# Two matmuls with a GELU between: b's first load cut in two, a first cast on two engines, and warm-up zeros from a constant

## The chip, the cores and the metric

The kernel runs on one NeuronCore of a Trainium2 chip. A core has a matrix engine (TensorE, PE in the profile; its weight loads are listed apart as PEld), a vector engine (VectorE, DVE), a scalar engine for activation functions (ScalarE, ACT), a general engine (GpSimd, POOL), a queue engine that here only issues transfers (SyncE, SP), and 16 DMA engines. The engines run their own instruction streams and wait for each other through semaphores. The metric is device time in microseconds (us), the median of several executions; less is better. A profiled execution has a span, from its first to its last instruction, and its own time, which is a little longer.

## The reference

```
h   = a @ b                      # a: 1024 x 1024, b: 1024 x 2048, float32
h   = 0.5*h*(1 + tanh(sqrt(2/pi)*(h + 0.044715*h**3)))
out = h @ c                      # c: 2048 x 1024, float32
```

## The kernel before

The order of all work is written out by hand: each engine does its instructions in the order in which the program lists them.

**Storage.** a comes to the core as float32 into `sta`, b's first 512 columns as float32 into `stb`; the rest of b and all of c come through POOL's queue, which converts them to bfloat16 on the way. The k axis (1024) is cut into eight slices of 128; `stb[:, k]` is slice k of b's first 512 columns, 256 KB.

**Loads.** All SP loads are issued at the start, in the order a piece, b pair, a piece, and again (lines 69 to 82). `load_a(h, q)` brings rows 512h to 512h + 511 of a and its columns 256q to 256q + 255; `load_b(q)` brings the two slices 2q and 2q + 1 of b. Each is 512 KB. `load_a(0, 0)`, `load_b(0)`, `load_a(1, 0)` are the first three. POOL's loads wait for a later piece of a through the one-element copy `gate` (line 84).

**Warm-up.** `stir` (lines 113 to 117) multiplies a tile of zeros, `warm`, with itself on PE, in passes of the given widths, into a PSUM bank that the first true product overwrites. It keeps PE at work while nothing has landed. `warm` is written by a DVE memset on line 50. A single-element Gelu on line 85 makes ACT load its table early.

**First stage.** For each piece of a, `cast_a` (119 to 125) converts float32 to bfloat16 (`ab`), on one or two engines, each taking a share of the 256 columns; `turn` (127 to 134) transposes it on PE in two groups of four and copies each group to `aT` with DVE. The second group goes to the same PSUM bank as the first. `cast_b` (136 to 139) converts a slice of b on ACT into `b1`, slice 0 in two halves. `block` then issues products of 128x512 on PE (line 105) for a row half, a set of column tiles and a set of slices. For the first pieces the order on PE is (lines 214 to 226):

```
stir(256, 256, 256, 256)
tn = turn(0, 0, 4, cast_a(0, 0, nc.vector))
next(tn)
stir(256)
next(tn)
stir(128)
cast_b(0, 2)
cast_b(1)
ab = cast_a(1, 0, nc.vector, nc.scalar)
block(0, range(4), (0,))
block(0, range(2), (1,))
tn = turn(1, 0, 7, ab)
next(tn)
```

So the six first products come before the transposes of a's second piece, and those before everything that follows.

**Later stages.** The other columns of the first matmul and the whole second one are done by a scheme with seven block products in place of eight (`Seven`, `seven`, lines 147 to 383): DVE forms sums and differences of blocks, PE multiplies them (line 197), DVE and ACT bring the results out of PSUM. `done2` stores the tiles of the output; the four tiles of the first quadrant go out in two halves each (line 443).

Of the kernel before, what the change touches and what calls it, by code (L numbers as in the profile page):

```python
# [9 lines left out]
F32 = mybir.dt.float32  # L10
F32R = mybir.dt.float32r
BF16 = mybir.dt.bfloat16
AF = mybir.ActivationFunctionType
# [6 lines left out]
def kernel(ctx, tc, a, b, c, out):  # L20
    nc = tc.nc
# [3 lines left out]
    H = 512  # L25
# [4 lines left out]
    bv = b.rearrange("(kt p) n -> p kt n", p=128)  # L30
# [3 lines left out]
    consts = ctx.enter_context(tc.tile_pool(name="consts", bufs=1))  # L34
# [5 lines left out]
    def slot(tag, shape, dt, name):  # L40
        return big.tile(shape, dt, name=name, tag=tag)

    def bank(i, shape=(128, H), dt=F32, name="ps"):
        return pp.tile(list(shape), dt, name=name, tag=f"bank{i}", padded_shape=None)

    def pieces(tag, bufs, shape, dt, name):
        return small.tile(shape, dt, name=name, tag=tag, bufs=bufs)

    warm = consts.tile([128, 256], F32, name="warm")
    nc.vector.memset(warm, 0.0)  # L50
    ident = consts.tile([128, 128], BF16, name="ident")
    make_identity(nc, ident)
    gate = consts.tile([128, 1], F32, name="gate")
    g = consts.tile([128, 1], F32, name="g")
# [11 lines left out]
    stb = slot("x0", [128, KT, H], F32, "stb")  # L66
    sta = [slot(f"x{i}", [128, 2, 2, 4, 256], F32, "sta") for i in (1, 3)]

    def load_a(h, q):
        nc.sync.dma_start(out=sta[q // 2][:, h, q % 2],  # L70
                          in_=av[:, 4 * h:4 * h + 4, ds(q * 256, 256)])

    def load_b(q):
        nc.sync.dma_start(out=stb[:, 2 * q:2 * q + 2], in_=bv[:, 2 * q:2 * q + 2, 0:H])

    load_a(0, 0)
    load_b(0)
    load_a(1, 0)
    for q in range(1, 4):
        load_a(0, q)  # L80
        load_b(q)
        load_a(1, q)

    nc.gpsimd.tensor_copy(gate, sta[1][:, 1, 0, 3, 0:1])
    nc.scalar.activation(g, warm[:, 0:1], AF.Gelu_apprx_tanh)


    for k in range(0, KT, 4):
# [1 line left out]
    for n in range(2):  # L90
        for k in range(0, KT, 4):
            nc.gpsimd.dma_start(out=b2[:, k:k + 4, ts(n, H)],
                                in_=bv[:, k:k + 4, ds(1024 + n * H, H)])
# [3 lines left out]
    def copy(eng, dst, src):  # L97
        if eng is nc.scalar:
            nc.scalar.activation(dst, src, AF.Copy)  # L99
        else:  # L100
            nc.vector.tensor_copy(dst, src)  # L101
# [11 lines left out]
    def stir(*widths):  # L113

        for w in widths:
            nc.tensor.matmul(ps[0, 3][:, 0:w], warm[:, 0:128], warm[:, 0:w],
                             start=True, stop=True, skip_group_check=True)

    def cast_a(h, q, *engs):

        ab = pieces("ab", 2, [128, 4, 256], BF16, "ab")
        for i, eng in enumerate(engs):
            w = 256 // len(engs)
            copy(eng, ab[:, :, ts(i, w)], sta[q // 2][:, h, q % 2][:, :, ts(i, w)])
        return ab

    def turn(h, q, i, ab):

        pt = bank(i, (128, 2, H), BF16, "pt")
        for n in range(2):  # L130
            for m in range(4):
                nc.tensor.transpose(pt[:, n, ts(m, 128)], ab[:, m, ts(n, 128)], ident)  # L132
            nc.vector.tensor_copy(aT[:, h, 2 * q + n], pt[:, n])  # L133
            yield

    def cast_b(k, n=1):
        for i in range(n):
            r = ds(i * (H // n), H // n)
            nc.scalar.activation(b1[:, k, r], stb[:, k, r], AF.Copy)  # L139
# [71 lines left out]
    zero = Seven(4, quarters(b1, H, 256), BB, [None] * 4, [None] * 4, 2)  # L211
    one = Seven(4, quarters(b2, 0, H), BB, [None] * 4, zero.t)

    stir(256, 256, 256, 256)
    tn = turn(0, 0, 4, cast_a(0, 0, nc.vector))
    next(tn)
    stir(256)
    next(tn)
    stir(128)
    cast_b(0, 2)  # L220
    cast_b(1)
    ab = cast_a(1, 0, nc.vector, nc.scalar)
# [2 lines left out]
    tn = turn(1, 0, 7, ab)  # L225
# [9 lines left out]
    tn = turn(0, 1, 7, ab)  # L235
# [8 lines left out]
    tn = turn(1, 1, 7, ab)  # L244
# [6 lines left out]
    tn = turn(0, 2, 7, ab)  # L251
# [8 lines left out]
    tn = turn(1, 2, 7, ab)  # L260
# [6 lines left out]
    tn = turn(0, 3, 7, ab)  # L267
# [13 lines left out]
    tn = turn(1, 3, 0, ab)  # L281
# [153 lines left out]
    def store(mt, q0, w, ot, eng=None):  # L435
        (eng or nc.sync).dma_start(out=out[ts(mt, 128), ds(q0, w)], in_=ot)

    def done2(i, l, j, p):
        if (i, l) == (1, 0):
            ot = pieces("o", 4, [128, H], F32, "ot")  # L440
            nc.vector.tensor_copy(ot, p)
            p = ot
        n = 2 if (i, l) == (0, 0) else 1
        for q in range(n):
            r = ds(q * (H // n), H // n)
            store(4 * i + j, l * H + q * (H // n), H // n, p[:, r])

    def between2(n):
# [12 lines left out]
        elif n == "P73":  # L461
            two.t4(two.t[1], 4)

    seven(two, done2, between2)


# [28 lines left out]
```

## Time and profile before

| | |
|---|---|
| Median of 13 runs | 118.22 us (117.94 to 119.35) |
| Profiled execution, its own time | 118.2 us |
| Its span | 116.4 us |
| PE busy | 111.1 us, 95% of the span |
| DVE busy | 90.5 us, 78% |
| ACT busy | 59.4 us, 51% |
| POOL busy | 11.0 us, 9% |
| SP's loads of a | 8 of 512 KB, 8.5 us from issue to landing |
| SP's loads of b | 4 of 512 KB, 8.1 us from issue to landing |
| First warm-up pass on PE | at 1.19 us |
| First product of the reference on PE | at 7.06 us |

A busy time is the sum over an engine's instructions; two engines are usually busy at once, so the rows don't add up to the span. The end of a PE instruction is modelled, and a busy PE isn't PE at its peak. A row of the trace gives start, length, engine, line, operation, operands, and in brackets the idle time of the engine before it with what ended that. The lines of the text are those of the kernel before.

### The profile page before, as it was taken

What the parts mean: (1) busy time and instruction counts of PE and PEld (TensorE: products, weight loads), DVE (VectorE), ACT (ScalarE), POOL (GpSimd) and SP (SyncE); (2) the same over time, 40 slices, a digit from 0 to 9 for tenths busy, and PEclk for the clock granted to TensorE, in tenths of its full rate; (3) what the DMA queues carried; (4) which work ended last, traced back from release to release, by engine and by line L of the source; (5) the groups of instructions that cost most, each with busy time, mean ns of one, the idle gap of its engine ahead of it and who ended that gap; (6) DMA issues with size and microseconds to landing.
All of it is one profiled execution on the core that took longest, in us unless ns stands there. A gap on an engine that the chain in (4) does not pass through costs nothing.

```text
span 116.4 us, 1478 instructions
## 1 busy us (share of the span) xinstructions
PE 111.1 (95%) x540; PEld 76.3 (66%) x540; DVE 90.5 (78%) x107; ACT 59.4 (51%) x99; POOL 11.0 (9%) x21
## 2 busy tenths in 40 slices
PE   5889999999999999999999999999999999999980
PEld 5544455545777447888886444588888888888860
DVE  0236666899998999844689999999999986954670
ACT  5066668989369898066699329600033982000000
POOL 2000049623322000000000000000000000000000
PEclk9999999999999999999999999999999999999999
DMA  3999999999999999997000000070000002014993
GB/s 87 292 376 391 395 395 312 204 207 207 204 210 213 211 212 210 212 210 150 3 0 0 0 6 0 2 268 0 0 0 0 0 0 96 0 63 174 368 361 115
DMA packets 13542, 17.91 MB, mean 154 GB/s; under 512 B 736, under 2 KB 8928, under 8 KB 13536
## 3 DMA queue, kind: packets, MB, share of 16 engines
q0 software_dynamic: 5344, 7.34, 35.5%
q1 hardware_dynamic: 8192, 10.49, 25.2%
q8 instruction: 4, 0.07, 0.2%
q14 instruction: 2, 0.02, 0.0%
HBM read 20.97 MB, written 4.19 MB: 216 GB/s over the span
## 4 chain that ended last, share of the span: by engine, by line
PE 91%; DMA 5%; DVE 1%; SPq 0%; ACT 0%; issue 0%
PE ps L197 76%; PE ps L105 12%; DMA stb<-in_b_dram 5%; PE pt L132 3%; DVE aT L133 0%; SPq L70 0%; ACT b L139 0%; DVE ot L382 0%
## 5 line engine op out<-in xcount | busy, mean ns | idle before, releaser
L197 PE MATMUL ps<-x,s 128*128 128x512 f32 x128 | 29.6, 391 | 0.0
L197 PEld LDWEIGHTS ps<-x,s 128*128 128x128 f32 x128 | 24.0, 188 | 5.1
L197 PE MATMUL ps<-x,x 128*128 128x512 f32 x96 | 22.9, 394 | 0.0
L197 PEld LDWEIGHTS ps<-x,x 128*128 128x128 f32 x96 | 18.0, 188 | 3.9
L105 PE MATMUL ps<-aT,b 128*128 128x512 bf16 x64 | 16.3, 379 | 0.3 <-ACT b L139 0.3
L305 ACT ACTIVATE v<-ps 128x512 f32<-128x512 f32 x10 | 6.0, 599 | 19.4 <-PE ps L197 19.4
L197 PE MATMUL ps<-c_sb,hT 128*128 128x512 bf16 (+1 forms) x72 | 14.2, 356 | 0.0
L197 PE MATMUL ps<-x 128*128 128x512 f32 x56 | 13.2, 392 | 0.0
L197 PEld LDWEIGHTS ps<-x 128*128 128x128 f32 x56 | 10.2, 188 | 2.6 <-ACT v L305 0.4
L197 PEld LDWEIGHTS <-hT 128*128 128x128 bf16 x72 | 6.9, 98 | 7.1 <-issue 0.5
L133 DVE COPY aT<-pt 128x512 bf16<-128x512 bf16 x16 | 6.8, 424 | 5.8 <-PE pt L132 5.8
L109 ACT ACTIVATE hT<-ot 128x512 bf16<-128x512 f32 x18 | 10.5, 625 | 1.5 <-DVE ot L310 1.1
L310 DVE TENSOR_TENSOR ot<-ps,v 128x512 f32<-128x512 f32 x10 | 6.7, 688 | 5.2 <-DMA out_dram<-ot 3.8
L310 DVE TENSOR_TENSOR ot<-ps,u 128x512 f32<-128x512 f32 x10 | 6.7, 691 | 5.1 <-ACT u L305 5.1
L197 PE MATMUL ps<-aT,b 128*128 128x512 bf16 x48 | 10.7, 379 | 0.0
L155 DVE TENSOR_TENSOR x<-c_sb 128x1024 fp32r<-128x1024 bf16 x8 | 9.3, 1225 | 0.0
L105 PEld LDWEIGHTS <-b 128*128 128x128 bf16 x64 | 5.5, 98 | 4.6 <-ACT b L139 0.9
L197 PEld LDWEIGHTS <-b 128*128 128x128 bf16 x48 | 4.6, 98 | 5.7 <-issue 0.3
L132 PEld LDWEIGHTS <-ab 128*128 128x128 bf16 x64 | 4.5, 97 | 5.9 <-DVE ab L101 2.1
L99 ACT ACTIVATE ab<-sta 128x512 bf16<-128x512 f32 x10 | 6.0, 625 | 3.5 <-DMA sta<-in_a_dram 3.4
L305 ACT ACTIVATE u<-ps 128x512 f32<-128x512 f32 x10 | 5.9, 598 | 3.3 <-PE ps L197 3.2
L109 ACT ACTIVATE hT<-ps 128x512 bf16<-128x512 f32 x14 | 7.3, 596 | 0.4 <-PE ps L105 0.3
(39 smaller groups left out, 114.3 us busy)
## 6 DMA issues: line engine op xcount, KB each, us to landing
sta<-in_a_dram SPq DMA_DIRECT2D x8, 512.0 KB, 8.5
c_sb<-in_c_dram POOLq DMA_DIRECT2D x8, 512.0 KB, 19.9
b<-in_b_dram POOLq DMA_DIRECT2D x6, 512.0 KB, 11.4
out_dram<-ot SPq DMA_DIRECT2D x12, 256.0 KB, 2.1
stb<-in_b_dram SPq DMA_DIRECT2D x4, 512.0 KB, 8.1
out_dram<-ot SPq DMA_DIRECT2D x8, 128.0 KB, 2.0
```

The costliest lines, as they stand in the source:

```text
L99: nc.scalar.activation(dst, src, AF.Copy)
L105: nc.tensor.matmul(p, b1[:, k, ts(t, 128)], aT[:, h, k], start=(k == 0), stop=(k == KT - 1))
L109: nc.scalar.activation(hT[h][:, t], p, AF.Gelu_apprx_tanh)
L132: nc.tensor.transpose(pt[:, n, ts(m, 128)], ab[:, m, ts(n, 128)], ident)
L133: nc.vector.tensor_copy(aT[:, h, 2 * q + n], pt[:, n])
L155: nc.vector.tensor_tensor(out=dst[:, r], in0=x[:, r], in1=y[:, r], op=op)
L197: nc.tensor.matmul(p[:, ds(c0, w)], l[:, k, ts(j, 128)], r[:, k, ds(c0, w)], start=(start and k == 0), stop=(k == self.kt - 1), skip_group ...
L305: nc.scalar.activation(st, p, AF.Copy)
L310: nc.vector.tensor_tensor(out=ot, in0=p, in1=st, op=ADD)
```

## The change

b's first load becomes two loads of one slice each, on the same queue; the warm-up reads its zeros from a constant that the program has anyway, so that tile and memset go; the table-loading Gelu stands ahead of the loads in the program; the first cast of a is shared by DVE and ACT; the warm-up passes have other widths; and the first output tile is stored whole.

```diff
-    warm = consts.tile([128, 256], F32, name="warm")
-    nc.vector.memset(warm, 0.0)
+    warm = nc.const_aps.tensor(0.0, [128, 256], F32)
...
+    def load_b0(k, eng):
+        eng.dma_start(out=stb[:, k], in_=bv[:, k, 0:H])
+
     def load_b(q):
         nc.sync.dma_start(out=stb[:, 2 * q:2 * q + 2], in_=bv[:, 2 * q:2 * q + 2, 0:H])
 
+    nc.scalar.activation(g, warm[:, 0:1], AF.Gelu_apprx_tanh)
     load_a(0, 0)
-    load_b(0)
+    load_b0(0, nc.sync)
+    load_b0(1, nc.sync)
     load_a(1, 0)
...
     nc.gpsimd.tensor_copy(gate, sta[1][:, 1, 0, 3, 0:1])
-    nc.scalar.activation(g, warm[:, 0:1], AF.Gelu_apprx_tanh)
...
-    stir(256, 256, 256, 256)
-    tn = turn(0, 0, 4, cast_a(0, 0, nc.vector))
-    next(tn)
-    stir(256)
+    stir(256, 256, 256, 256, 128)
+    tn = turn(0, 0, 4, cast_a(0, 0, nc.vector, nc.scalar))
     next(tn)
     stir(128)
+    next(tn)
+    stir(64)
     cast_b(0, 2)
...
-        n = 2 if (i, l) == (0, 0) else 1
+        n = 2 if (i, l) == (0, 0) and j else 1
```

## The prediction

> **What bounds the kernel now.** I read the busy row first, then the chain of waits in order of time, then the first 17 us engine by engine, because every edit but one lies there.
>
> The slices of the page say that TensorE (PE) is busy nearly all the time, while the DMA engines are full through about the first 23 us:
>
> ```profile
> PE   5889999999999999999999999999999999999980
> DMA  3999999999999999997000000070000002014993
> ```
>
> The chain that ended last gives the work on the path. Its pieces (start, length, what) include:
>
> ```profile
> 1.22 5.35 DMA stb<-in_b_dram
> ...
> 7.06 1.47 PE ps L105 x6
> ...
> 25.16 87.99 PE ps L197 x400
> ```
>
> Read naively this says: 5.35 us wait on b's first load, then nothing but PE to 113.2 us, so every tenth by which b comes sooner is a tenth off the end. The chain names only one releaser per step, however. I ask what the next wait would be if this one went, and read VectorE (DVE) and ScalarE (ACT) in the same stretch (start, length, line, operation, idle time before it and what ended it):
>
> ```profile
> 4.46 0.69 DVE L101 CAST ab<-sta 128x1024 bf16<-128x1024 f32 x1 [3.33 <-DMA sta<-in_a_dram]
> 5.64 0.42 DVE L133 COPY aT<-pt 128x512 bf16<-128x512 bf16 x1 [0.49 <-PE pt L132]
> 6.54 0.42 DVE L133 COPY aT<-pt 128x512 bf16<-128x512 bf16 x1 [0.47 <-PE pt L132]
> 7.95 0.43 DVE L101 CAST ab<-sta 128x512 bf16<-128x512 f32 x1 [0.98 <-DMA sta<-in_a_dram]
> ```
>
> The last row decides this case. DVE has been idle 0.98 us when it casts the second piece of a (rows 512 to 1023, load_a(1, 0)): that piece has only just landed, near 7.93. Its first transpose follows at once:
>
> ```profile
> 8.43 0.23 PEld L132 LDWEIGHTS <-ab 128*128 128x128 bf16 x4 [0.39 <-DVE ab L101]
> ```
>
> 7.95 + 0.43 = 8.38, and PE takes the cast piece at 8.43. So two chains meet at 8.4: b's first load through six products, and a's second piece through its cast. They are a tie. Later pieces of a gate PE too, by little:
>
> ```profile
> 9.63 1.15 ACT L99 ACTIVATE ab<-sta 128x512 bf16<-128x512 f32 x2 [1.06 <-DMA sta<-in_a_dram]
> 12.23 0.63 ACT L99 ACTIVATE ab<-sta 128x512 bf16<-128x512 f32 x1 [0.25 <-DMA sta<-in_a_dram]
> 16.28 0.63 ACT L99 ACTIVATE ab<-sta 128x512 bf16<-128x512 f32 x1 [0.27 <-DMA sta<-in_a_dram]
> ```
>
> PE transposes from these casts at 10.32, 12.71 and 16.78. What runs ahead of each is three, five and five products of 0.216 us (1.08 us for five in the chain): 9.56 + 0.65 = 10.21, 11.51 + 1.08 = 12.59, 15.67 + 1.08 = 16.75. PE therefore stands still for 0.11, 0.12 and 0.03 us, and could not gain more by being early. Up to about 16.8 us the clock of this kernel is the stream of loads; from there on it is PE's own work.
>
> That stream, by stretches of 1.5 us (PE, PEld, DVE, ACT and POOL busy, granted clock, DMA share, GB/s), is not even:
>
> ```profile
> 2.75:4.25 1.50, 1.50 (x5) 1.22 (x4) 0.00 (x0) 0.00 (x0) 0.00 (x0) 1.00 1.08 363
> 4.25:5.75 1.50, 1.02 (x8) 0.52 (x7) 0.80 (x2) 0.00 (x0) 0.00 (x0) 1.00 0.89 224
> 5.75:7.25 1.50, 1.19 (x9) 0.64 (x8) 0.74 (x2) 0.66 (x3) 0.00 (x0) 1.00 1.05 360
> 7.25:8.75 1.50, 1.50 (x11) 0.67 (x10) 0.43 (x1) 1.22 (x3) 0.00 (x0) 1.00 1.08 391
> ```
>
> While b's first load moves, the rate drops to 224 GB/s although the engines stay 0.89 busy. Against 391 that is (391 - 224) x 1.5 us = 250 KB, or 0.64 us. I cannot say why; it matters below.
>
> **What the skill says.** "DMA: Bandwidth & Descriptors", section "Queues, rings and completion order": on each DMA engine the descriptors of one queue are consumed in ring order, and a load's semaphore step lands after all earlier writes of that engine. The trace agrees: a's first piece, b's first load and a's second piece are waited for until 4.44, 6.57 and 7.93, in the order of issue. "Perfetto Trace Analysis", section "DMA Optimizations": splitting helps some work start sooner if the engines are generally idle. Here they are full, so the split only decides which bytes of b come first. "TensorE: Matmul & The Clock Gate", Part 1: PE starts at half rate, comes to full rate after about 3.4 us of activity, and may fall back after an idle window of that length. The trace agrees on the first half: eight passes of the warm-up take 3.55 us, two later ones of the same size 0.65 us, and no fall back shows. "ScalarE: Activation LUTs", "What ACT_TABLE_LOAD costs": 186 ns plus 0.833 ns an element, 613 ns for 512; the casts here take 613 to 630.
>
> **The change part by part.**
>
> *b's first load in two.* 512 KB become two loads of 256 KB on SP, slice k = 0 ahead. At 4.25 us the stream has moved 129 x 1.55 + 363 x 1.5 = 745 KB; slice 0 ends at 786 KB, so at 224 GB/s its data are in by 4.45. b's whole load (1,048 KB) is in by the same sum at 5.6 and is waited for until 6.57, one microsecond for the landing. Slice 0 then lands near 5.45, slice 1 near 6.57 as before.
>
> *First cast on two engines.* DVE does 128x512 in 0.43 instead of 128x1024 in 0.69, ACT the other half in 0.63: 4.46 to 4.89 and to 5.09. ACT is free, as it was idle 4.36 us up to 6.59. First transposes 0.26 sooner, at 4.94; the first aT copy ends near 5.80 instead of 6.06. The second group of transposes waits for that copy (same bank, as before), near 5.85.
>
> *Warm-up.* DVE's memset (0.27) goes, and PE need not wait until 1.19; the other engines start at 0.73, so PE gains some 0.4. Four 256-wide passes cost 3.55, the added 128-wide one half of 0.89, together 4.0: from 0.8 to 4.8, inside the wait for the first cast. The two later ones shrink by half, which saves about 0.2 each, hidden. Reading zeros from a broadcast constant isn't shown in the trace; I take the same rate, with 1 us more as the bad end, which the slack below covers in part.
>
> *Sum for the first product.* PE is through its second transposes and the small warm-up near 6.3; b's slice 0 is cast 5.47 to 6.25. First product near 6.35, not 7.06: 0.7 sooner. Slice 1 is cast 6.59 to 7.22, its first two products end near 7.7. Then PE reaches the transposes of a's second piece, which lands at 7.93 as before: it waits to 8.43. Of 0.7 us nearly all is lost in that wait. What remains is the bit by which PE was itself late at 8.43, at most 0.05.
>
> *SP's queue.* One issue more, 0.43 to 0.49 each; everything behind it (a's second piece and the rest) is issued some 0.4 later. a's second piece would be issued by about 2.7, and its first bytes move only after 1,048 KB, at 5.6, so 2.9 us of queue hide it. For later loads 8 us lie between issue and landing. Cost taken as 0; bounds 0 to +0.4.
>
> *The rest.* The Gelu that loads the activation table moves ahead of nothing on ACT (next work at 4.46, table and Gelu done at 2.22): 0. The first output tile goes out as one 256 KB store, not two: one SP issue of 0.35 less at 75 us, under a single unbroken PE piece from 25.16 to 113.15: 0. The removed tile shifts later addresses by 1 KB; nothing in the trace prices that: 0, bounds -0.1 to +0.1.
>
> Sum: -0.05 on a profiled span of 116.4, whose execution took 118.2 (1.8 outside the span) and is the median of 118.22 to within 0.02. Forecast 118.15.
>
> **The rivals.**
>
> *Faster: the stream itself gains.* The drop at 4.25 to 5.75 belongs to b's first load. If two loads of consecutive rows don't suffer it, or less, a's second piece lands up to 0.64 sooner, and since every later gate is a landing, all of it arrives at the end: 117.5 to 117.85. For it: the drop lies exactly on the load that is cut, and b's later loads ran at 391. Against: the bytes, row sizes and row pitch are the same.
>
> *Faster: the naive chain.* The full 0.7 would count, 117.5. The cast at 7.95 speaks against it.
>
> *Slower: PE's clock falls back.* Between 4.8 and 8.43 PE now works less: transposes 0.46, warm-ups 0.35, six products 1.3, some 2.1 of 3.6 us, where before it was some 2.6 of 3.7. If that counts as idle, products run at half rate for a window of 3.4 us after 8.43: up to +1.7, 119.2 to 119.9. It decides from the point where that stretch is under the limit; the trace shows none. One of the thirteen times before is 119.35, which such a fall back could explain.
>
> *Slower: the extra load delays the stream* by one issue, 0.4, if the DMA engines run dry behind it: 118.6.
>
> *It doesn't do what it says*, slice 0 landing with slice 1: also 118.2.
>
> **How the numbers follow.** About 0.3% (0.35 us) is what a measurement of this kernel can tell from no change. No change 0.42 (118.0 to 118.4 for its own part). Faster 0.36: stream 0.30, naive chain 0.06. Slower 0.22: clock 0.10, stream 0.12. The range 117.5 to 118.9 holds the stream's gain and loss and leaves out mostly the clock.
>
> **What would show it.** First product near 6.35; DVE's cast of a's second piece again near 7.95 after more than a microsecond of idle, and the six products no longer touching the transposes at 8.43; the cast pieces at 9.6, 12.2 and 16.3 in place. I am wrong if that cast starts 0.3 or more away from 7.95, either way: the end will move with it. If it stays and the end moves, the tie was misread, or PE's rate changed after 8.4.

## The result and the profile after

The changed kernel is slower: a median of 119.5 us (118.84 to 120.42, 11 runs) against 118.22 us (48 runs). The ratio is 1.0106, with a 95% interval of 1.0089 to 1.0123. Its profiled execution took 118.84 us with a span of 117.0 us. That is its fastest run, so the profile shows 0.64 us of a loss that is 1.28 us in the median. What it shows of the place holds, of the size only the lower part. In e6, e9, e10, e13 and e18 below, the executions that are some 2 to 4 us longer than the others of their kernel, with a lower clock of PE, are left out of the ratio and counted in the median.

The slices of the page after (same rows as shown of before):

```profile
PE   7968999999999999999999999999999999999980
DMA  3999999999999999999000000070000002014993
```

A slice is 2.9 us. PE is busier than before in the first two (7 and 9 instead of 5 and 8) and idler in the third and fourth (6 and 8 instead of 8 and 9), and the DMA engines stay full a little longer. The chain of waits in order of time (start, length, what) has another long wait:

```profile
2.23 6.53 DMA sta<-in_a_dram
...
8.78 0.44 DVE ab L104
...
25.77 88.02 PE ps L200 x400
```

The long wait is no longer on b but on the second piece of a. The long PE piece is as long as before (88.02 against 87.99 us) and starts 0.61 us later. The loss is complete before 25.77 us. DVE and ACT in the first stage (start, length, line, operation, idle time before and what ended it):

```profile
4.09 0.43 DVE L104 CAST ab<-sta 128x512 bf16<-128x512 f32 x1 [4.09 <-DMA sta<-in_a_dram]
...
8.78 0.43 DVE L104 CAST ab<-sta 128x512 bf16<-128x512 f32 x1 [2.45 <-DMA sta<-in_a_dram]
```

```profile
6.47 0.72 ACT L142 ACTIVATE b<-stb 128x256 bf16<-128x256 f32 x2 [1.75 <-DMA stb<-in_b_dram]
7.42 0.63 ACT L142 ACTIVATE b<-stb 128x512 bf16<-128x512 f32 x1 [0.23 <-DMA stb<-in_b_dram]
8.78 0.63 ACT L102 ACTIVATE ab<-sta 128x512 bf16<-128x512 f32 x1 [0.73 <-DMA sta<-in_a_dram]
...
12.88 0.63 ACT L102 ACTIVATE ab<-sta 128x512 bf16<-128x512 f32 x1 [0.28 <-DMA sta<-in_a_dram]
16.90 0.63 ACT L102 ACTIVATE ab<-sta 128x512 bf16<-128x512 f32 x1 [0.28 <-DMA sta<-in_a_dram]
```

The cast of a's second piece starts at 8.78, not 7.95; the casts that stood at 12.23 and 16.28 start at 12.88 and 16.90. PE has a long wait where the tie was:

```profile
9.27 0.40 PE L135 MATMUL pt<-ident,ab 128*128 128x128 bf16 x4 [0.56 <-DVE ab L104]
```

So the stream of loads is late, and PE follows. The windows of 1.5 us (columns as in the prediction, GB/s last) show where:

```profile
2.75:4.25 1.50, 1.50 (x6) 1.21 (x5) 0.16 (x1) 0.16 (x1) 0.00 (x0) 1.00 1.08 272
4.25:5.75 1.50, 1.26 (x14) 0.96 (x12) 0.69 (x2) 0.47 (x1) 0.00 (x0) 1.00 0.78 176
5.75:7.25 1.50, 0.65 (x7) 0.33 (x5) 0.42 (x1) 0.72 (x2) 0.00 (x0) 1.00 0.99 311
7.25:8.75 1.50, 1.33 (x6) 0.30 (x4) 0.00 (x0) 0.63 (x1) 0.00 (x0) 1.00 1.07 371
```

Before had 363, 224, 360 and 391 GB/s. With the window from 1.20 (129 before, 165 after, 1.55 us), 2,207 KB had moved by 8.75 us before and 1,951 KB now. The missing 256 KB take 0.65 us at 392 GB/s, the mean of both from 8.75 to 11.75 us. That is what the end lost: the last DVE addition that PE feeds is at 113.82, not 113.17.

PE's clock has no part in this execution: four transposes last 0.40 us at 9.27, as they did at 8.43 before. (The column of the granted clock alone doesn't prove it; see e15 below.) In two of the twelve recorded executions of the change, of 120.42 and 119.43 us, the mean granted clock was 0.984 and 0.980, and there it may add to the loss. The six at 0.999 or more took 118.84 to 119.66 us, so the loss stands without it.

### The profile page after: what moved, and what is told of

Read it like the earlier page. It is cut to its first block, busy times and chain, and to the rows that moved or that the text cites. A ratio compares the mean times of both kernels' runs of the same rounds, so it can differ in the third digit from the quotient of the medians.

```text
span 117.0 us, 1483 instructions
## 1 busy us (share of the span) xinstructions
PE 111.2 (95%) x542; PEld 76.7 (66%) x542; DVE 89.7 (77%) x106; ACT 60.1 (51%) x100; POOL 11.0 (9%) x21
## 4 chain that ended last, share of the span: by engine, by line
PE 89%; DMA 6%; SPq 1%; DVE 1%; issue 0%
PE ps L200 75%; PE ps L108 10%; DMA sta<-in_a_dram 6%; PE pt L135 3%; SPq L73 1%; DVE ab L104 0%; DVE aT L136 0%; DVE ot L385 0%; SPq L69 0%
## 5 line engine op out<-in xcount | busy, mean ns | idle before, releaser
L102 ACT ACTIVATE ab<-sta 128x512 bf16<-128x512 f32 x11 | 6.6, 625 | 5.8 <-DMA sta<-in_a_dram 5.8
```

## The experiments

All kernels below are `before` with one edit, except e2, which is the changed kernel with one edit undone. The theory to be tested is that cutting b's first load costs the time; its rivals were another part of the change, PE's clock, and, once the cut was found, other reasons for which a cut may cost. The expectations state each theory beside its number.

One table first, because two separate costs have to be kept apart. "Cast" is where the cast of a's second piece starts in the profiled execution. "PE part" is how much later than 113.17 us the last DVE addition starts. "Tail" is the span less that start. Rows are left out where PE's clock had also fallen in the profiled execution (e5, e9, e10, e12, e13, e18), and for e7, which puts b's load first.

A profiled execution is one of several, and not always a typical one: that of the change is its fastest; those of e8 (119.47 us), e13 (122.02) and e15 (120.33) are the slowest of their kernels. Apart from e5, e7 and e15, a's first piece is cast between 4.09 and 4.72 us in the profiled executions, mostly with nothing changed ahead of it. Differences of some 0.3 us between two single profiles therefore say little.

| kernel | median us | ratio to before | cast | PE part | tail |
|---|---|---|---|---|---|
| before | 118.22 | | 7.95 | | 3.2 |
| the change | 119.5 | 1.0106 | 8.78 | +0.65 | 3.2 |
| e1 cut alone | 119.72 | 1.0128 | 9.51 | +1.35 | 3.7 |
| e2 all but the cut | 118.24 | 1.0004 | 8.18 | +0.05 | 3.3 |
| e3 cut by columns | 119.39 | 1.0118 | 9.10 | +0.89 | 3.6 |
| e11 cut in four | 119.81 | 1.0151 | 9.12 | +0.99 | 3.6 |
| e4 tiny load on ACT | 118.67 | 1.0044 | 8.34 | +0.10 | 3.6 |
| e6 second b load cut | 118.87 | 1.0040 | 8.07 | +0.23 | 3.7 |
| e8 issues held back | 118.49 | 1.0026 | 8.97 | +0.86 | 3.7 |
| e14 tiny load after b | 118.65 | 1.0058 | 8.09 | -0.12 | 3.6 |
| e15 tiny load first | 119.1 | 1.0101 | 8.53 | +1.71 | 3.7 |
| e16 a's second piece late | 118.10 | 0.9991 | 8.21 | -0.02 | 3.2 |
| e17 b late by 0.08 | 118.22 | 0.9998 | 8.12 | -0.02 | 3.2 |

Two readings. The PE part is the delay of the cast less 0.2 to 0.3 us: the tie of the prediction, with that much cushion. Two rows stand apart. e6 delays a later piece (cast at 12.51, not 12.23). In e15 the first piece of a was late too (cast at 5.14, not 4.46), and PE ran slowly until about 10 us: two warm-up passes took 1.17 us there against 0.65 before, and six products 2.15 against 1.47, while the clock column of the windows reads 1.00. The durations decide. And the tail has two values. It is 3.2 to 3.3 us in the eight kernels that issue no more transfers from SP and ACT than `before` (it, the change, e2, e7, e13, e16, e17, e18) and 3.6 to 3.7 in the twelve that issue at least one more. The wait of SP at the end of the program shows it, before and in e1 (engine, line, waited for: us in total, times, longest):

```profile
SPq L490 <- DMA out_dram<-ot: 1.1, 2, 0.8
```

```profile
SPq L491 <- DMA out_dram<-ot: 1.5, 1, 1.5
```

A possible reason: in the traces the transfers of SP and ACT land on eight completion semaphores in turn, the last store of `before` and of the change on number 7, that of e1 on number 0. If the end waits for them in order, a last store on number 0 leaves seven more to pass, one on number 7 none. That is a reading; no run was made for it, and e11, whose last store has number 2, has the same tail. The +0.4 itself has no exception in twenty kernels. The change adds a load and takes a store away, so it pays none of it. Of the losses of e4, e6 and e14 it is most, and of e1's about a quarter.

### Which part costs it: e1 and e2

e1, the cut alone:

```
-    load_b(0)
+    for k in range(2):
+        nc.sync.dma_start(out=stb[:, k], in_=bv[:, k, 0:H])
```

> The kernel before with one edit: b's first load is two loads of one slice. Theory A (taking b's rows slice after slice makes the load stream slower): the loss of the whole change comes from here alone, a's second piece lands near 8.8 instead of 7.93, ratio 1.005 to 1.013. Theory B (one of the other edits disturbs the stream: zeros from the constant, the shared cast, the moved Gelu or the 1 KB shift): ratio 1.000, a's second piece near 7.9. Theory C (one more issue on SP starves the stream): as A, with SP's later issues 0.4 to 0.5 us later.

119.72 us (119.11 to 120.09, 6 runs), ratio 1.0128 [1.0105, 1.0152]. Windows of e1, the two that differ most from before:

```profile
4.25:5.75 1.50, 0.89 (x7) 0.29 (x5) 0.69 (x1) 0.00 (x0) 0.00 (x0) 1.00 0.79 152
5.75:7.25 1.50, 1.47 (x13) 0.88 (x10) 0.85 (x2) 0.72 (x2) 0.00 (x0) 1.00 0.89 264
```

The slow stretch, 224 then 360 GB/s in `before`, is 152 then 264.

e2, the change with b's first load whole:

```
-    load_b0(0, nc.sync)
-    load_b0(1, nc.sync)
+    load_b(0)
```

> The changed kernel with b's first load as one load again, all other edits kept. A and C: back to the time before, ratio 0.997 to 1.002, a's second piece near 7.9. B: the loss stays, ratio near 1.010.

118.24 us (117.96 to 118.38, 13 runs), ratio 1.0004 [0.9996, 1.0012]. Windows of e2:

```profile
4.25:5.75 1.50, 1.23 (x9) 0.79 (x8) 0.85 (x2) 0.63 (x1) 0.00 (x0) 1.00 0.86 235
5.75:7.25 1.50, 0.70 (x7) 0.56 (x7) 0.43 (x2) 0.56 (x2) 0.00 (x0) 1.00 1.06 365
```

The rates are those of `before`. All other edits together are worth nothing, and the cut carries the loss.

### What about the cut: e3, e11, e6

e3 cuts the load by columns, so that each half still reads both slices; e11 cuts it in four; e6 leaves it whole and cuts the next load of b.

```
# e3
-    load_b(0)
+    for c0 in (0, 256):
+        nc.sync.dma_start(out=stb[:, 0:2, c0:c0 + 256], in_=bv[:, 0:2, c0:c0 + 256])
# e11: for k in range(2): for c0 in (0, 256): stb[:, k, c0:c0 + 256]
# e6: load_b(1) becomes one load for each of the slices 2 and 3
```

> The kernel before, b's first load as two loads of 256 columns each, both slices in each: the same bytes and the same one more issue on SP, but rows of both slices alternate as before, in pieces of 1 KB. A: ratio 0.998 to 1.003, the rate between 4.25 and 5.75 us stays near 224 GB/s or rises. C: ratio near 1.010, as with the split by slices.

> The kernel before, b's first load as four loads: two slices, each in two halves of 256 columns. C and K by number of pieces: three extra loads where the changed kernel has one, ratio 1.02 to 1.04, a's second piece near 10 or later. If only the first cut matters: ratio 1.009 to 1.015.

> The kernel before, b's first load whole, its second load (slices 2 and 3, the fifth load on SP) as two of one slice. C and E as costs of every load: ratio 1.005 to 1.012. H (only loads whose data move in the first 6 us or so suffer): ratio 0.999 to 1.002, and the slices 2 and 3 move at 390 to 415 GB/s.

e3: 119.39 us (119.05 to 120.38, 6 runs), 1.0118 [1.0090, 1.0146]. e11: 119.81 (119.53 to 120.36, 4 runs), 1.0151 [1.0119, 1.0183]. e6: 118.87 (118.52 to 121.29, 7 runs), 1.0040 [1.0023, 1.0057]. The order of the rows alone is not the cause, as e3 loses too; its windows:

```profile
4.25:5.75 1.50, 1.47 (x8) 0.62 (x7) 0.98 (x2) 0.42 (x1) 0.00 (x0) 1.00 0.79 214
5.75:7.25 1.50, 1.26 (x9) 0.58 (x7) 0.57 (x2) 0.07 (x1) 0.00 (x0) 1.00 0.67 194
```

The loss doesn't grow with the number of pieces: three more loads (e11) delay the PE part by 0.99 us, one more by 0.89 and 1.35. And it is not a price of any cut: in e6 the cut load moves at full rate (393 GB/s in 8.75:10.25), PE is 0.23 us late, and the rest is the tail.

### What belongs to b: e4, e7, e18, e8

e4 touches b early with 8 KB on ACT's queue; e7 loads b ahead of both pieces of a, e18 after both; e8 puts a small copy that waits for a's first piece behind the fourth load, so that later issues are held back.

```
# e4, ahead of load_a(0, 0)
+    nc.scalar.dma_start(out=room, in_=bv[:, 0, H:H + 16])
# e7: load_b(0), load_a(0, 0), load_a(1, 0)      e18: load_a(0, 0), load_a(1, 0), load_b(0)
# e8, after the fourth load
+            nc.sync.dma_start(out=room, in_=sta[0][:, 0, 0, 0, 0:16])
```

> The kernel before with one tiny load from b (128 rows of slice 0, 64 bytes each, into an unused tile) issued on ACT's queue ahead of everything. Theory D (the drop of the stream is a price of the first reads from b, paid whenever they come): the drop at 4.25 to 5.75 us shrinks as it is paid beside a's first load, a's second piece lands up to 0.6 us sooner, ratio 0.995 to 0.999. A and C: the drop stays, ratio 1.000 to 1.002.

> The kernel before with b's first load issued ahead of a's first piece. If the drop of the stream belongs to b's rows, it moves to the first load, and a's first piece then runs at 350 to 390 GB/s. If it belongs to the second load or to the time after 4 us, b comes quickly (waited for until about 4.4) and a's first piece falls into the drop. Ratio 0.998 to 1.004 in either case, as the third load lands at the same time.

> The kernel before with b's first load behind a's second piece, third on the queue and issued near 1.76. If the slow reads go with b's rows: the second load runs at 360 to 395 GB/s and the drop comes with the third, from about 5 us. If they go with the second load: the drop falls on a's second piece from 4 us, and b runs at 390. The time says little, as the first product waits for b until 8 us or later and PE's clock may fall back: ratio 1.01 to 1.04.

> The kernel before, with a 64 byte per partition copy from a's first piece put on SP's queue after the fourth load: it waits for that piece to land, so no load is issued from about 3 to 4.5 us. Theory F (the drop is a price of SP issuing more loads while the stream runs): the drop shrinks, a's second piece lands 0.2 to 0.6 us sooner, ratio 0.995 to 0.999. C and H: the drop stays, ratio 1.000 to 1.004.

e4: 118.67 us (118.48 to 118.71, 5 runs), 1.0044 [1.0032, 1.0056], and the slow stretch stays (255 GB/s). An early touch of the rows of slice 0 cures nothing; those of slice 1 were not touched. e7: 121.62 us (121.29 to 121.99, 4 runs), 1.0284 [1.0259, 1.0309], far above the 0.998 to 1.004 expected: a's first piece came so late that PE stood still for 2.56 us until 7.52, and then ran slowly as in e15 (two passes 1.17 us). e18: 119.24, 121.54, 122.0 and 122.17, only the first without a fall of PE's clock, too few for a ratio. The rates answer the question, not the times: the slow stretch goes with b. e7 and then e18:

```profile
2.75:4.25 1.50, 1.50 (x5) 1.23 (x4) 0.00 (x0) 0.00 (x0) 0.00 (x0) 1.00 0.92 233
4.25:5.75 1.50, 0.72 (x2) 0.00 (x0) 0.00 (x0) 0.39 (x2) 0.00 (x0) 1.00 0.99 335
```

```profile
4.25:5.75 1.50, 1.50 (x7) 0.80 (x6) 0.80 (x2) 0.00 (x0) 0.00 (x0) 1.00 1.01 349
5.75:7.25 1.50, 1.33 (x8) 0.77 (x7) 0.68 (x3) 0.00 (x0) 0.00 (x0) 1.00 0.88 223
```

With b first, the low rate (233) is in the first full window; with a's second piece in b's place, that piece runs at 349 GB/s and the low rate comes one window later. It isn't the second place in the queue that is slow but the first rows of b. e8: 118.49 us (118.33 to 119.47, 20 runs), 1.0026 [1.0011, 1.0042]. The stretch stays at 240 GB/s with no issue from 2.8 to 4.4 us, so that later issues crowd it isn't the reason; 0.3 us is less than the added tail.

### An extra load, or the lateness: e10, e14, e15, e9

e10, e14 and e15 add the same 8 KB load of a to SP's queue: between a's first piece and b, after b, and ahead of everything. e9 cuts a's first piece and leaves b whole.

```
+    nc.sync.dma_start(out=room, in_=av[:, 0, 0:16])     # e10, e14, e15
# e9
-    load_a(0, 0)
+    for m in (0, 2):
+        nc.sync.dma_start(out=sta[0][:, 0, 0, m:m + 2], in_=av[:, m:m + 2, 0:256])
```

> The kernel before with one tiny load from a (128 rows, 64 bytes each, into an unused tile) on SP between a's first piece and b's first load, which stays whole. C: ratio 1.005 to 1.013 though no load was cut. K: ratio 0.999 to 1.003, with 8 KB more to move and one issue of 0.4 to 0.5 us more.

> The kernel before with the tiny load of 8 KB from a on SP behind b's first load and ahead of a's second piece: b is issued at 1.22 as before, a's second piece near 2.25. N: ratio above 1.005, as in the change. P for b's issue alone: ratio 0.999 to 1.003.

> The kernel before with the tiny load ahead of a's first piece: every load is issued 0.45 to 0.5 us later, the start of the stream too. N: ratio above 1.008. P: only the start moves, ratio 1.003 to 1.005, with the drop as long as before.

> The kernel before, a's first piece as two loads of 256 KB, b's first load whole. Theory C (each extra load among the first costs): a's second piece lands 0.5 us or more later than 7.93, ratio 1.005 to 1.015. Theory K (only cutting b's first rows costs, because the slow reads are there): ratio 0.999 to 1.003.

e10: 118.97, 120.41, 122.11 and 123.39 us, 1.0136 [1.0061, 1.0210] from the first two; cast at 10.17. e14: 118.65 (118.27 to 119.65, 10 runs), 1.0058 [1.0031, 1.0085]. e15: 119.1 (118.96 to 120.33, 4 runs), 1.0101 [1.0051, 1.0151]. e9: 119.04, 122.26, 122.49 and 123.26; cast at 10.51. Windows of e10:

```profile
4.25:5.75 1.50, 1.42 (x7) 0.70 (x7) 0.74 (x2) 0.00 (x0) 0.00 (x0) 1.00 0.73 181
5.75:7.25 1.50, 1.49 (x8) 0.94 (x7) 0.63 (x2) 0.00 (x0) 0.00 (x0) 1.00 0.87 264
```

b's load is whole here, only issued at 1.78 instead of 1.22, and its stretch is as slow as in e1. So b need not be cut for the loss. The same 8 KB behind b (e14) leave cast and PE part alone in the profiled execution (118.48 us). Six of e14's ten executions are 118.27 to 118.66, which the tail alone accounts for; four are 119.16 to 119.65, none of them profiled, so a further cost of an added load isn't excluded. In e15 three of four are 118.96 to 119.10, some 0.8 us above `before`: about the tail's 0.4 and the 0.43 us by which everything is issued later (an estimate from these two figures). The fourth, the profiled one, is the one with the slow PE.

### Lateness with no extra load: e13, e16, e17

SP can be made to wait for a DVE memset of the buffer that a load is about to fill. e13 delays b's first load that way, e16 a's second piece, e17 b's first load by a shorter memset.

```
+    nc.vector.memset(stb[:, 0, 0:512], 0.0)             # e13, ahead of load_b(0)
+    nc.vector.memset(stb[:, 0, 0:128], 0.0)             # e17
# e16, ahead of load_a(1, 0)
+    for m in range(4):
+        nc.vector.memset(sta[0][:, 1, 0, m], 0.0)
```

> The kernel before, b's first load waiting on SP for a DVE memset of its slice 0, so that it is issued near 1.75 us as in the run with the tiny load between, with no load added. Theory P (a load that is issued late against the start of the stream at about 2 us moves slowly): the slow stretch lasts beyond 6 us, a's second piece lands 0.5 us or more after 7.93, ratio above 1.005. Theory N (the number of loads on the queue): the drop is as before, ratio 0.999 to 1.003.

> The kernel before, a's second piece waiting on SP for DVE memsets into its tile, so that it is issued near 2.25 us as in the change, with no load added and b whole. P for the second piece's issue: the slow stretch lasts beyond 6 us, ratio above 1.005. N: ratio 0.999 to 1.003.

> The kernel before, b's first load waiting for a DVE memset of a quarter of its slice 0, so that it is issued near 1.4 us, about 0.2 late and without an additional load. P as a smooth dependence: about 0.4 of the loss of the longer delay, ratio 1.002 to 1.005. P as an edge near 1.7 us: ratio 0.999 to 1.002. No dependence: the same.

e13: 119.43 us (118.62 to 122.02, 7 runs), 1.0077 [1.0048, 1.0107]. e16: 118.10 (117.89 to 118.43, 12 runs), 0.9991 [0.9981, 1.0000]. e17: 118.22 (118.11 to 118.33, 13 runs), 0.9998 [0.9986, 1.0009]. SP's issue of b and the windows in e13:

```profile
1.71 0.38 SPq L74 DMA_DIRECT2D stb<-in_b_dram  x1
```

```profile
4.25:5.75 1.50, 1.40 (x7) 0.68 (x6) 0.72 (x2) 0.00 (x0) 0.00 (x0) 1.00 0.67 170
5.75:7.25 1.50, 1.14 (x8) 0.74 (x7) 0.82 (x2) 0.00 (x0) 0.00 (x0) 1.00 0.90 284
```

Half a microsecond of lateness of one unaltered load, with no transfer added and a tail of 3.2 us, makes a slow stretch like that of the cut (170 and 284 GB/s). In `before` the DMA engines are 0.89 and 1.05 busy in these windows, here 0.67 and 0.90, although SP had issued b and the two next pieces of a by 3.15 us. Dividing rate by busy share, 170/0.67 = 254 is what `before` has with 224/0.89 = 252: the engines that work are no slower than there, but more of them stand idle. Windows of e16:

```profile
4.25:5.75 1.50, 1.50 (x7) 0.80 (x6) 0.80 (x2) 0.00 (x0) 0.00 (x0) 1.00 0.83 248
5.75:7.25 1.50, 1.50 (x8) 1.10 (x8) 0.54 (x2) 0.68 (x3) 0.00 (x0) 1.00 0.88 276
```

a's second piece, issued at 2.26 instead of 1.76, costs nothing, and the memsets as such don't either. e17 moved b's issue to 1.30 only, 0.08 us where 0.2 was intended: that costs nothing, and where between 0.08 and 0.5 us the loss begins isn't known.

### Other ways to bring slice 0 first: e5, e12

e5 issues slice 1 on ACT's queue; e12 puts a's second piece between the slices.

```
# e5
-    load_b(0)
+    nc.sync.dma_start(out=stb[:, 0], in_=bv[:, 0, 0:H])
+    nc.scalar.dma_start(out=stb[:, 1], in_=bv[:, 1, 0:H])
# e12: load_a(0, 0), slice 0, load_a(1, 0), slice 1, all on SP
```

> The kernel before, b's first load in two slices, the second issued on ACT's queue. Theory C (one more load or issue on SP's queue at the start is what costs): SP has its old number of loads, ratio 0.998 to 1.003, a's second piece near 7.9. Theory E (pieces of 256 KB in place of 512 KB cost whichever queue issues them): ratio 1.008 to 1.013. Theory H (the first loads suffer together, and two in flight at once suffer more): ratio above 1.004.

> The kernel before, b's first load cut in two slices as in the change, with a's second piece issued between them. If what gates the end is only the landing of a's second piece, that lands 0.3 to 0.7 us sooner than in the split alone and the ratio is 1.003 to 1.008. If the slow reads of b set back all loads behind them alike, later pieces of a are as late as in the split alone, ratio 1.008 to 1.014.

e5: 121.86 us (121.67 to 121.92, 4 runs), 1.0301 [1.0286, 1.0316]. "DMA: Bandwidth & Descriptors" of the Trainium skill, section "Issuing engines are not separate DMA queues", says that transfers of different engines run on the same 16 DMA engines and interleave. They do, and here that is the harm: slice 1, issued on ACT's queue at 0.73 us, shares the engines with a's first piece, issued on SP's at 0.74, and that piece, cast at 4.46 before, is cast at 6.97. PE waits, and its clock falls. First the transposes of e5, then its windows:

```profile
7.73 0.61 PE L133 MATMUL pt<-ident,ab 128*128 128x128 bf16 x4 [3.14 <-DVE ab L102]
```

```profile
7.25:8.75 1.50, 1.02 (x6) 0.94 (x7) 0.80 (x2) 0.95 (x3) 0.00 (x0) 0.58 1.08 382
8.75:10.25 1.50, 1.50 (x9) 1.11 (x8) 0.54 (x3) 0.92 (x2) 0.00 (x0) 0.50 1.07 401
```

e12: 121.35 us (120.57 to 122.03, 4 runs), 1.0274 [1.0212, 1.0336]. a's second piece is cast at 8.03 as in `before`, but slice 1 is now what PE lacks: it is waited for until 9.76, where in `before` the whole of b's first load was in by 6.57; PE's clock then falls here too (0.50 from 10.25 to 11.75 us), so the ratio holds both:

```profile
9.78 0.63 ACT L140 ACTIVATE b<-stb 128x512 bf16<-128x512 f32 x1 [2.53 <-DMA stb<-in_b_dram]
```

No version tried is clearly faster than `before`; e16, the best, has 1.0000 in its interval.

## Why the prediction was wrong

**The tie was read rightly.** The prediction tied the end to the landing of a's second piece and named that cast as the place to look: 0.3 or more away from 7.95, and the end moves with it. It moved by 0.83 and the end by 0.65. PE's earlier start brought nothing (e2: first transposes 0.32 us sooner than before, ratio 1.0004). The naive chain, which would have paid out an earlier first product in full, doesn't fit e3, where that product starts 0.62 us sooner than the 7.06 of before and the end is still 0.89 us later:

```profile
6.44 0.60 PE L106 MATMUL ps<-aT,b 128*128 128x512 bf16 x2
```

**The step that failed is the one headed "SP's queue".** "Cost taken as 0; bounds 0 to +0.4." The argument was that 2.9 us of queued bytes hide one more issue of 0.4 us. The bytes did hide the issue of a's second piece (e16: 0.9991 with the same lateness). But b itself is not hidden by the bytes queued ahead of it: cut, or issued 0.5 us later, its slow stretch, which the prediction had measured as 0.64 us and left unexplained, becomes longer (e1, e13). The missing 256 KB are 0.65 us in the profiled execution; the median has lost 1.28 us, three times the upper bound. What the bound assumed, that a later issue can cost at most its own lateness, is false for this load (e13: 0.5 us late, cast 2.4 us later in its profiled execution, the slowest of seven; the four in the ratio lose 0.9 us).

**The rivals.** "The stream itself gains" (0.30 of the chances) had the right stretch and the wrong sign. What spoke against it, "the bytes, row sizes and row pitch are the same", was read as a reason for no gain; it is none against a loss. "The extra load delays the stream" (0.12) had the right place, but its price of 0.4 was that of an issue. Its condition, engines that run dry, is in part what the windows show: from 4.25 to 5.75 us they are 0.89 busy before, 0.78 in the change and 0.67 in e13. The fall of PE's clock (0.10) didn't occur in the changed kernel's profile. e5 shows that it is real: after 3.14 us without work PE's clock was 0.58 and then 0.50. "TensorE: Matmul & The Clock Gate", Part 1, of the Trainium skill puts the idle window at about 3.4 us. The measured waits are shorter: in e10 one of 2.05 us was followed by a clock of 0.50.

```profile
9.29 1.08 PE L106 MATMUL ps<-aT,b 128*128 128x512 bf16 x4 [2.05 <-ACT b L140]
10.25:11.75 1.50, 1.50 (x8) 0.75 (x7) 0.41 (x2) 0.65 (x2) 0.00 (x0) 0.50 1.07 385
```

The change's own waits before its products and transposes are 0.85 and 0.56 us. So this rival was nearer than the prediction's reading of the page allowed, and e5, e9, e10, e12, e13 and e18 paid for it.

**Landings of b.** Slice 0 was to land near 5.45 and was waited for until 6.45; slice 1 near 6.57, until 7.40. At the rates measured after, 165 x 1.55 + 272 x 1.5 = 664 KB have moved by 4.25 us, and slice 0 (786 KB) is in at 4.25 + 122/176 = 4.94, not 4.45. The other 0.5 us is in the step from there to the landing, taken as 1 us from a whole load; by the same sum it comes out as 1.5. The first product is at 6.94, not 6.35.

**What was right, at zero.** The first cast on two engines, the passes of the warm-up from a constant (ten in 3.86 us from 0.77, no slower each than the eight in 3.55 before), the Gelu ahead, the moved addresses: all inside e2's 1.0004 [0.9996, 1.0012].

**Right for a wrong reason.** The whole output store was costed at 0 because one issue of 0.35 us at 75 us is hidden. It is, but the number of transfers isn't free: with the cut and without the whole store (e1) the tail is 0.4 us longer.

**The skill's advice.** "Perfetto Trace Analysis" of the Trainium skill, section "DMA Optimizations", has splitting help where DMA engines are generally idle. The prediction used it to call the split neutral on full engines. The trace goes further: in the window of 4.25 to 5.75 us the busy share fell from 0.89 to 0.78 with the cut and the rate from 224 to 176 GB/s. It wasn't neutral.

**What stays open.** Why b's first rows are read at 223 to 255 GB/s when a's second piece isn't (a's first bytes are slow too, 164 GB/s from 2.25 to 2.50 us in `before`, but for half a microsecond only), and why a cut or a later issue makes it worse. In the change itself slice 0 was issued at 1.21 as before and only slice 1 half a microsecond later (1.76), yet the rate is already lower from 2.75 us on (272 against 363), with the engines as busy as before (1.08). There the engines work but are slower, as they are in e1 from 4.25 us (152/0.79 = 192 against 252), which is not what e13 shows. Whether the lateness of slice 1 alone, or the cut as well, does this isn't settled.

## What to carry to other kernels

Where the stream of loads is the clock of a stage, look for the next landing that gates before you credit an earlier start, and don't take an added or later issue among the first loads as free because bytes are queued ahead of it: an unexplained slow stretch in the stream is a risk in both directions, and a run of that one edit prices it. Read the tail of the span apart from the rest, since a transfer more or less anywhere can shift it. Judge PE's clock by how long equal instructions last, and not by the clock column alone. When an edit brings several parts, undo the suspected one in the changed kernel and do it alone in the old one, and expect the two not to add up exactly.

## What the runs showed of the hardware that was not expected

The first rows of b, loaded whole, come at 223 to 255 GB/s wherever they stand in the queue (233 as the first load in e7, 224 to 255 as the second in before, e2, e4, e6, e8, e14, e16 and e17, 223 as the third in e18), against 349 for a's second piece in b's place and 393 while a later load of b moves (e6). Issued 0.5 us later, unaltered, they held the stream at 170 and 284 GB/s, with the engines 0.67 and 0.90 busy (e13). A transfer more on SP's or ACT's queue lengthened the end of the program by 0.4 us in twelve of twelve kernels. Moving half of a load from SP's to ACT's queue delayed another transfer, issued on SP's at the same moment, by 2.5 us (e5). PE's clock fell to 0.50 after a wait of 2.05 us (e10). And PE can run slowly (two passes 1.17 us for 0.65) while the clock column reads 1.00 (e15, e7).
